# A gather of one activation is issued ahead of each added row, twelve rows ahead, in the v stage of a PEER layer

## The chip, the cores and the metric

The kernel runs on one core of a Trainium2 chip. The metric is the device time of one execution, in microseconds (us). TensorE is called PE here, its weight loads PEld, VectorE DVE, ScalarE ACT, GpSimd POOL and SyncE SP.

## The reference

A decoder trunk of two layers over 256 tokens of width 1024. Each layer is a mixer followed by a PEER feed-forward block, each behind a layer norm. Only the PEER block is touched. Per token it chooses 8 x 16 of 16384 experts; each expert has a row of `u` and a row of `v`, 1024 floats each:

```python
u_e = u[experts]
v_e = v[experts]
a = jax.nn.gelu(jnp.einsum("thkd,td->thk", u_e, xc), approximate=False)
return jnp.einsum("thk,thkd->td", (g * a).astype(v.dtype), v_e)
```

`experts` are the chosen indices, `g` their softmax weights.

## The kernel before

`peer(l)` runs once for each of the two layers. Its two long stages treat all experts densely, 128 of them a step:

- The **u stage** (128 steps) streams `p_u` and computes the activation of every expert for every token. For 192 of the 256 tokens these stay in the chip's memory and are multiplied there by the gates. For the last 64 tokens (`GT`) they go to a scratch table in device memory, `actD`, by a store of POOL every fourth step (line 735).
- The **v stage** (the loop over `j` at line 820, 128 steps) streams `p_v`, 512 KB a step, and multiplies it by the gated activations of those 192 tokens.

The 64 other tokens have 8 x 16 chosen experts each, 8192 (token, expert) pairs, laid out as 64 columns of 128 pairs. For each column c POOL issues two indirect DMAs: `g_act(c)` (line 456) gathers 128 single floats, the activations, from `actD` into one column of a small tile `gel`; `g_row(c)` (line 450) gathers 128 rows of `p_v`, 4 KB each, so 512 KB, into one of a ring of six tiles (`RING`). `g_mac(c)` (line 460) is DVE's: at every fourth column it multiplies four columns of `gel` by the gates into `gw` (line 462), then it adds row times weight to `gacc` (line 467), and then it has POOL issue `g_row(c + 6)` into the tile that it has just freed. The first six rows are gathered while the u stage runs.

In a v step, in program order: `nxt` prepares tiles two or three steps ahead (SP loads a `p_v` tile into one of eight buffers, `raw` or `spare`, line 92; ACT rounds it to `hi`, line 104; DVE subtracts for `lo`, line 115), `w_lo` and `w_hi` split the activations in the same way (lines 751 and 746), then the gathers and `g_mac` come, and last `v_mm`, ten matmuls of 128x512 (line 181; for the last eight steps four of the ten are put off to the end of the stage). A load into a buffer waits until DVE has finished with the tile that is in it, eight tiles back. Each engine works through its own list in program order.

Which step does what for the gathered columns: at step 0 `g_act(0)` to `g_act(3)` are issued, and at each step j from 1 to 60 `g_act(j + 3)`. The column gc is added at step 7 + int(113/64 x gc), so one column every 1.77 steps: column 0 at step 7, column 30 at step 59, column 51 at step 97, column 63 at step 118.

Of the kernel before, what the change touches and what calls it, by code (L numbers as in the profile page):

```python
# [35 lines left out]
GT = 64  # L36
ND = S - GT
RING, LEAD = 6, 7
GB = 0.8
GS = 2.0 ** 15  # L40


class Kern:
# [379 lines left out]
    def peer(self, l):  # L423
        tc, nc, I = self.tc, self.nc, self.I
        self.v0 = self.v0s.pop(0)
        with ExitStack() as es:
# [23 lines left out]
            def g_row(c):  # L450
                if c < P // 2:
                    t = grow[c] = gat.tile([P, D], F32, tag="row", name="row", bufs=RING)
                    nc.gpsimd.indirect_dma_start(out=t, out_offset=None, in_=gtable,  # L453
                                                 in_offset=bass.IndirectOffsetOnAxis(ap=gidx[:, 0, c:c + 1], axis=0))

            def g_act(c):
                nc.gpsimd.indirect_dma_start(out=gel[c // 4][:, c % 4:c % 4 + 1], out_offset=None, in_=gplaces,  # L457
                                             in_offset=bass.IndirectOffsetOnAxis(ap=gidx[:, 1, c:c + 1], axis=0))

            def g_mac(c):  # L460
                if c % 4 == 0:
                    nc.vector.tensor_tensor(gw[:, c:c + 4], gel[c // 4], ggate[:, c:c + 4], op=OP.mult)
                t = grow.pop(c)
                if c == 0:
                    nc.vector.tensor_scalar(gacc, t, gw[:, 0:1], None, op0=OP.mult)
                else:
                    nc.vector.scalar_tensor_tensor(gacc, t, gw[:, c:c + 1], gacc, op0=OP.mult, op1=OP.add)  # L467
                g_row(c + RING)
# [143 lines left out]
            def g_flush(n=1):  # L612
                if len(gq) < n:
                    return
                while gq:
                    t0, oi, gs = gq.popleft()
                    ps = self.acc(t0 // 4 % 2)
                    for q in range(4):
                        for w in range(2):
                            self.mm(ps[:, q * P:(q + 1) * P], oi[:, q // 2, :, q % 2], gs[w][:, q // 2, :, q % 2],  # L620
                                    w == 0, w == 1)
                    pv = ps.rearrange("p (t j) -> p j t", t=4)
                    k = done["a"]
                    for x, j0, n in A:
                        m = min(max(k, 0), n)
                        if m > 0:
                            y = x[:, 0:m, t0:t0 + 4]
                            nc.vector.scalar_tensor_tensor(y, pv[:, j0:j0 + m], 1.0 / GS, y, op0=OP.mult, op1=OP.mult)  # L628
                        if m < n:
                            nc.scalar.activation(x[:, m:n, t0:t0 + 4], pv[:, j0 + m:j0 + n], AF.Copy, scale=1.0 / GS)  # L630
                        k -= n
                    done["g"] = t0 + 4
# [3 lines left out]
            def run_side(budget):  # L636
                credit[0] = min(credit[0] + budget, 2 * budget)
                while credit[0] > 0 and side:
                    try:
                        cost = next(side[0])  # L640
                        if cost is None:
                            return
                        credit[0] -= cost
                    except StopIteration:
                        side.popleft()
# [67 lines left out]
            def u_fin(x):  # L713
                while due:
                    y, ps = due.popleft()
                    nc.vector.tensor_tensor(y, y, ps, op=OP.mult)
                if x is None:
                    return
                j, ps, wide = x
                jj = (P - FIRST + j) % P  # L720
                y, n = slot(jj), done["g"]
                if wide:
                    t = gat.tile([P, S], F32, tag="half", name="half", bufs=2)
                    nc.scalar.copy(t, ps[:, S:2 * S])  # L724
                    nc.vector.tensor_tensor(ps[:, 0:S], ps[:, 0:S], t, op=OP.add)  # L725
                if n:
                    nc.scalar.activation(ps[:, 0:n], ps[:, 0:n], AF.Gelu)  # L727
                    due.append((y[:, 0:n], ps[:, 0:n]))
                if n < ND:
                    nc.scalar.activation(y[:, n:ND], ps[:, n:ND], AF.Gelu)  # L730
                if j % 4 == 0:
                    gst.append(gat.tile([P, 4, GT], F32, tag="gst", name="gst", bufs=2))
                nc.scalar.activation(gst[-1][:, j % 4, :], ps[:, ND:S], AF.Gelu)  # L733
                if j % 4 == 3:
                    nc.gpsimd.dma_start(self.actD[:, jj - 3:jj + 1, :], gst.pop())  # L735
                done["a"] = j + 1
# [6 lines left out]
            def w_hi(j):  # L743
                if j < P:
                    WW[j] = late[0].tile([P, 3 * P], F32R, tag="w", name="W", bufs=10) if late else W[0][:, j % 5, :]
                    nc.scalar.copy(WW[j][:, 0:ND], slot(j))  # L746

            def w_lo(j):
                if j < P:
                    for o, c in ((2 * P, slice(0, P)), (ND, slice(P, ND))):  # L750
                        nc.vector.tensor_tensor(WW[j][:, o:o + c.stop - c.start], slot(j)[:, c],  # L751
                                                WW[j][:, c].bitcast(F32), op=OP.subtract)
# [8 lines left out]
            for j in range(P):  # L761
# [3 lines left out]
                g_flush(2)  # L765
                run_side(1.6 if len(A) == 1 else GB)
                if not side and len(A) == 1:
# [8 lines left out]
            while side or gq:  # L776
                g_flush()
                run_side(GB)
            u_fin(pu)
# [10 lines left out]
            def v_mm(j, tt, blocks, start=False, stop=False):  # L790
                hi, lo, w = kept[j]
                xh, xl, xm = w[:, 0:P], w[:, 2 * P:3 * P], w[:, P:2 * P]
                items = ((xm, hi), (xm, lo)) if tt else ((xh, hi), (xh, lo), (xl, hi))
                for a, (xx, ww) in enumerate(items):
                    go, end = start and a == 0, stop and a == len(items) - 1
                    for f in blocks:
                        self.mm(accs[tt][f], xx, ww[:, f * 512:(f + 1) * 512], go, end)

            rate, gc = (P - 8 - LEAD) / 64, 0
# [20 lines left out]
            for j in range(P):  # L820
                if j == P - FIRST:

                    es_1.close()
                    late.append(es.enter_context(tc.tile_pool(name="late", bufs=2 * NT - 6, reuse_waits="tile")))
                    for q in range(P - NT, P - 3):
                        self.alt[self.si + q - j] = lambda: [late[0].tile([P, D], F32R, tag="keep", name="keep") for _ in range(2)]
                hi, lo = self.nxt(j < P - 2)
                w_lo(j + 2)
                w_hi(j + 3)
                if j == NEXT + 1:  # L830
                    hN = self.reload_h()
                if j + 4 == P - 1:
                    gb = self.load_gb(2 * l + 1)
                kept[j] = (hi, lo, WW.pop(j))
                for c in range(4) if j == 0 else range(j + 3, min(j + 4, 64)):
                    g_act(c)
                if late_sums:
                    late_sums.popleft()()
                while gc < 64 and j >= LEAD + int(rate * gc):
                    g_mac(gc)  # L840
                    gc += 1
                    if gc in (60, 64):
                        late_sums.append((g_alpha, g_copy)[gc == 64])
                v_mm(j, 0, (0, 1), j == 0, j == P - 1)
                if j < P - NT:
                    v_mm(j, 1, (0, 1), j == 0)
                    kept.pop(j)
# [785 lines left out]
```

## Time and profile before

| | us |
|---|---|
| median of 3 runs (1788.25 to 1798.21) | 1792.02 |
| the profiled execution | 1791.22 |
| its span, first to last instruction | 1789.4 |
| v stage of layer 0, from | 557 |
| v stage of layer 1, from | 1468 |

The span is what the trace shows from the first to the last instruction. The two v stages are read by stretches of the trace: the stretches in which activations are gathered, and those after the last of these (710 us in layer 0, 1630 us in layer 1). Busy time of POOL holds its DMA issues as long as they take on the engine. "remote" as a releaser is an event from outside the engines; where the waiting instruction reads a loaded tile, it is the load.

### The profile page before, as it was taken

Reading aid. Unit: us, or ns where it says so; the run is one execution under the profiler, and the core shown is the slowest. Engines: PE = TensorE matmul, PEld = TensorE weight load, DVE = VectorE, ACT = ScalarE, POOL = GpSimd, SP = SyncE. Lnnn points to the kernel's source line nnn. Section 1 sums busy time; section 2 is a strip of 40 time slices with the busy share of each in tenths; the row PEclk is TensorE's granted clock in tenths of the full one; section 3 lists DMA queues with packets and bytes.
Section 4 is the critical chain, followed back from the end, with each engine's and each line's share of the span. In section 5 each row is a group of like instructions: output and inputs, shape, how many; then the busy total and the mean of one; then the engine's idle time right before and its main releaser. Section 6 shows DMA issues by size and latency. Waiting matters only on the chain. (4 is left out here: it accounts for less than half of the span.)

```text
span 1789.4 us, 30937 instructions
## 1 busy us (share of the span) xinstructions
PE 1730.8 (97%) x10610; PEld 1489.2 (83%) x10610; DVE 1554.7 (87%) x3675; ACT 1042.2 (58%) x2267; POOL 494.5 (28%) x441
## 2 busy tenths in 40 slices
PE   7999999999999999999897999999999999989997
PEld 6879999888888867888785789998888887768886
DVE  6778988989997989999768779988899987879998
ACT  6646455666666545556457755556666665445553
POOL 2110002000003777661431210020000007766630
PEclk9999999999999999999999999999999999999999
DMA  7445657555557999997671365666555558989992
GB/s 257 158 144 177 201 172 271 189 178 179 183 174 256 368 316 344 377 375 277 220 229 53 101 219 185 197 203 238 182 177 176 187 190 324 345 297 354 378 371 92
DMA packets 120654, 416.69 MB, mean 233 GB/s; under 512 B 18065, under 2 KB 20145, under 8 KB 119409
## 3 DMA queue, kind: packets, MB, share of 16 engines
q1 hardware_dynamic: 91008, 322.61, 53.6%
q0 software_dynamic: 29488, 92.10, 13.9%
q8 instruction: 84, 1.38, 0.3%
q14 instruction: 74, 0.60, 0.1%
HBM read 400.49 MB, written 13.63 MB: 231 GB/s over the span
## 5 line engine op out<-in xcount | busy, mean ns | idle before, releaser
L181 PE MATMUL mm<-hT,hi 128*128 128x256 f32 (+1 forms) x3360 | 838.6, 330 | 0.0
L181 PE MATMUL mm<-hT,lo 128*128 128x256 f32 x2376 | 638.2, 281 | 1.1 <-DVE lo L115 1.0
L104 ACT CAST hi<-raw 128x1024 fp32r<-128x1024 f32 (+1 forms) x463 | 484.2, 1048 | 255.2 <-PE acc L181 87.3
L115 DVE TENSOR_TENSOR lo<-raw,hi 128x1024 fp32r<-128x1024 f32 (+1 forms) x459 | 559.1, 1221 | 44.0 <-ACT hi L104 32.6
L181 PEld LDWEIGHTS mm<-hT,hi 128*128 128x128 f32 x3360 | 552.2, 188 | 49.3 <-issue 1.2
L181 PEld LDWEIGHTS mm<-hT,lo 128*128 128x128 f32 x2376 | 448.3, 189 | 15.5 <-DVE lo L115 1.9
L181 PE MATMUL acc<-hi,W 128*128 128x512 f32 x1476 | 419.6, 392 | 6.3 <-issue 4.7
L181 PEld LDWEIGHTS acc<-hi,W 128*128 128x128 f32 x1476 | 276.8, 188 | 71.5 <-issue 11.7
L181 PE MATMUL acc<-lo,W 128*128 128x512 f32 x984 | 307.3, 393 | 7.1 <-issue 4.7
L453 POOL DMA_INDIRECT row<-p_v,gidx x128 | 220.8, 1725 | 132.8 <-DVE gacc L467 90.7
L735 POOL DMA_DIRECT2D actD<-gst x64 | 34.9, 546 | 794.5 <-ACT gst L733 794.5
L181 PEld LDWEIGHTS acc<-lo,W 128*128 128x128 f32 x984 | 183.3, 188 | 54.8 <-issue 10.2
L104 ACT CAST hi<-spare 128x1024 fp32r<-128x1024 f32 x126 | 132.3, 1050 | 139.9 <-PE acc L181 101.7
L115 DVE TENSOR_TENSOR lo<-spare,hi 128x1024 fp32r<-128x1024 f32 x126 | 153.7, 1220 | 26.7 <-issue 16.9
L457 POOL DMA_INDIRECT gel<-actD,gidx x128 | 148.1, 1157 | 51.5 <-issue 37.8
L467 DVE SCALAR_TENSOR_TENSOR gacc<-row,gw,gacc 128x1024 f32<-128x1024 f32 x126 | 161.3, 1280 | 1.1
L727 ACT ACTIVATE mm<-mm 128x192 f32<-128x192 f32 (+23 forms) x170 | 40.9, 241 | 122.5 <-DVE mm L725 122.5
L751 DVE TENSOR_TENSOR W<-A,W 128x128 fp32r<-128x128 f32 (+1 forms) x512 | 107.5, 251 | 1.8 <-ACT W L746 1.8
L746 ACT CAST W<-A 128x192 fp32r<-128x192 f32 x256 | 88.3, 346 | 0.0
L725 DVE TENSOR_TENSOR mm<-mm,half 128x256 f32<-128x256 f32 x174 | 74.4, 428 | 15.1 <-ACT half L724 14.7
L628 DVE SCALAR_TENSOR_TENSOR A<-acc,A 128x176 f32<-128x176 f32 (+16 forms) x268 | 55.9, 274 | 34.7 <-PE acc L181 31.7
L730 ACT ACTIVATE A<-mm 128x192 f32<-128x192 f32 (+23 forms) x244 | 67.7, 277 | 7.1 <-DVE mm L725 2.0
(275 smaller groups left out, 1755.1 us busy)
## 6 DMA issues: line engine op xcount, KB each, us to landing
raw<-p_u SPq DMA_DIRECT2D x256, 512.0 KB
raw<-p_v SPq DMA_DIRECT2D x128, 512.0 KB
spare<-p_v SPq DMA_DIRECT2D x128, 512.0 KB
raw<-p_wq SPq DMA_DIRECT2D x32, 512.0 KB
actD<-gst POOLq DMA_DIRECT2D x64, 128.0 KB
raw<-b_wo SPq DMA_DIRECT2D x12, 512.0 KB
raw<-a_wo SPq DMA_DIRECT2D x8, 512.0 KB
raw<-s_wT SPq DMA_DIRECT2D x8, 512.0 KB
```

The costliest lines, as they stand in the source:

```text
L104: self.nc.scalar.copy(self.his[i], self.raws[i])
L115: e.tensor_tensor(self.los[i], raw, self.his[i].bitcast(F32), op=OP.subtract)
L181: self.nc.tensor.matmul(out, a, b, start=start, stop=stop)
L453: nc.gpsimd.indirect_dma_start(out=t, out_offset=None, in_=gtable, in_offset=bass.IndirectOffsetOnAxis(ap=gidx[:, 0, c:c + 1], axis=0))
L457: nc.gpsimd.indirect_dma_start(out=gel[c // 4][:, c % 4:c % 4 + 1], out_offset=None, in_=gplaces, in_offset=bass.IndirectOffsetOnAxis(ap=g ...
L467: nc.vector.scalar_tensor_tensor(gacc, t, gw[:, c:c + 1], gacc, op0=OP.mult, op1=OP.add)
L628: nc.vector.scalar_tensor_tensor(y, pv[:, j0:j0 + m], 1.0 / GS, y, op0=OP.mult, op1=OP.mult)
L725: nc.vector.tensor_tensor(ps[:, 0:S], ps[:, 0:S], t, op=OP.add)
L727: nc.scalar.activation(ps[:, 0:n], ps[:, 0:n], AF.Gelu)
L730: nc.scalar.activation(y[:, n:ND], ps[:, n:ND], AF.Gelu)
L746: nc.scalar.copy(WW[j][:, 0:ND], slot(j))
L751: nc.vector.tensor_tensor(WW[j][:, o:o + c.stop - c.start], slot(j)[:, c], WW[j][:, c].bitcast(F32), op=OP.subtract)
```

## The change

A constant `AHEAD = 12` is added, and the place of the activation gathers in the v loop is changed. The number of instructions and of DMAs stays, and so does the order of the rows.

```diff
-                for c in range(4) if j == 0 else range(j + 3, min(j + 4, 64)):
+                for c in range(2 * j, 2 * j + 2) if j < AHEAD // 2 else ():
                     g_act(c)
                 if late_sums:
                     late_sums.popleft()()
                 while gc < 64 and j >= LEAD + int(rate * gc):
+                    if gc + AHEAD < 64:
+                        g_act(gc + AHEAD)
                     g_mac(gc)
                     gc += 1
```

Steps 0 to 5 now issue two activation gathers each (columns 0 to 11), and from step 7 on one is issued ahead of each `g_mac`, for the column twelve further on; the last, column 63, at step 97.

## Rows read from the trace of the kernel before

**Rows 1.** Engines over the whole span: busy us (share) x instructions (page, part 1).
```profile
PE 1730.8 (97%) x10610; PEld 1489.2 (83%) x10610; DVE 1554.7 (87%) x3675; ACT 1042.2 (58%) x2267; POOL 494.5 (28%) x441
```

**Rows 2.** Matmul line 181, by stretch: length, PE, PEld busy (count), clock, DMA, GB/s.
```profile
557.00:640.00 83.00, 83.00 (x366) 68.29 (x365) 1.00 0.96 353
640.00:710.00 70.00, 65.55 (x269) 48.90 (x268) 1.00 0.92 322
710.00:840.00 130.00, 130.00 (x575) 107.62 (x575) 1.00 0.97 361
1490.00:1630.00 140.00, 131.00 (x535) 99.96 (x535) 0.98 0.90 317
1630.00:1760.00 130.00, 130.00 (x575) 107.65 (x574) 1.00 0.95 355
...
750.00:760.00 10.00, 10.00 (x46) 8.28 (x45) 1.00 1.01 406
...
1600.00:1610.00 10.00, 6.49 (x15) 3.69 (x16) 0.73 0.65 200
```

**Rows 3.** Timeline of PE, undisturbed stretch: start us, length us, instruction, count.
```profile
723.86 1.07 PE L181 MATMUL acc<-hi,W 128*128 128x512 f32 x4
...
726.13 1.07 PE L181 MATMUL acc<-hi,W 128*128 128x512 f32 x4
```

**Rows 4.** Waits, 640 to 710 us: total us, times, longest us.
```profile
ACT hi L104 <- remote: 8.9, 5, 3.1
```

**Rows 5.** Waits, 1490 to 1630 us.
```profile
ACT hi L104 <- remote: 22.8, 7, 6.6
```

**Rows 6.** Waits, 1630 to 1740 us: no activation gathers left.
```profile
ACT hi L104 <- PE acc L181: 47.3, 48, 2.0
POOL row L453 <- DVE gacc L467: 41.6, 26, 2.8
```

**Rows 7.** Timeline of layer 1, start of its v stage; idle before in brackets.
```profile
1489.41 0.16 DVE L462 TENSOR_TENSOR gw<-gel,ggate 128x4 f32<-128x4 f32 x1 [5.13 <-DMA gel<-actD,gidx]
...
1503.69 1.05 ACT L104 CAST hi<-spare 128x1024 fp32r<-128x1024 f32 x1 [6.60 <-remote]
```

**Rows 8.** Waits of SP's queue, 555 to 850 us.
```profile
SPq L92 <- DVE W L751: 205.4, 95, 4.5
```

**Rows 9.** Line 453 alone, 710 to 810 us: length, POOL busy (count), clock, DMA.
```profile
710.00:810.00 100.00, 67.70 (x26) 1.00 0.99 376
```

**Rows 10.** DMA of 640 to 710 us, then of 1490 to 1630 us.
```profile
DMA packets 7123, 22.55 MB, mean 322 GB/s; under 512 B 1632, under 2 KB 1632, under 8 KB 7117
...
gel<-actD,gidx POOLq DMA_INDIRECT x29
...
DMA packets 13780, 44.32 MB, mean 317 GB/s; under 512 B 3115, under 2 KB 3115, under 8 KB 13642
...
gel<-actD,gidx POOLq DMA_INDIRECT x56
```

**Rows 11.** Timeline of POOL: packed stretch, act-free stretch, the longest activation gather.
```profile
604.33 1.03 POOL L457 DMA_INDIRECT gel<-actD,gidx  x1 [0.30 <-DMA row<-p_v,gidx]
605.67 0.97 POOL L453 DMA_INDIRECT row<-p_v,gidx  x1 [0.30 <-issue]
...
741.04 3.51 POOL L453 DMA_INDIRECT row<-p_v,gidx  x1 [0.65 <-DVE gacc L467]
...
1574.88 3.85 POOL L457 DMA_INDIRECT gel<-actD,gidx  x1 [0.31 <-issue]
```

**Rows 12.** Busy us of all engines (instructions), clock, DMA share, GB/s: 580 to 600.
```profile
580.00:600.00 20.00, 20.00 (x90) 16.57 (x89) 19.96 (x34) 11.14 (x19) 15.92 (x15) 1.00 0.94 341
```

**Rows 13.** Groups of the page: count, busy us, mean ns, idle before and releaser.
```profile
L453 POOL DMA_INDIRECT row<-p_v,gidx x128 | 220.8, 1725 | 132.8 <-DVE gacc L467 90.7
...
L457 POOL DMA_INDIRECT gel<-actD,gidx x128 | 148.1, 1157 | 51.5 <-issue 37.8
```

More of the change, by code (lines that the diff above doesn't have):

```diff
@@ L38 @@
 RING, LEAD = 6, 7
+AHEAD = 12
 GB = 0.8
```

## The prediction

> **What bounds the kernel now.** I read the page's engine table first: PE is busy for 97% of the span, DVE for 87% [rows 1]. So time can only come from where PE stands still. The second view is the matmuls of line 181 by stretches of the two v stages [rows 2]. An undisturbed step takes PE 2.27 us, from the start of a group of four matmuls to that of the next step's [rows 3], so 0.227 us for each of its ten. At that pace 640 to 710 us would hold 308 matmuls and holds 269: 39 are missing, 8.9 us. 1490 to 1630 us would hold 617 and holds 535: 82 are missing, 18.6 us. The stretches after the last activation gather (710 to 840, 1630 to 1760) hold 575 in 130 us, which is the full pace, and so does 557 to 640. So PE loses 27.5 us in the two v stages, all of it while activations are being gathered. A part of the 18.6 us is the clock: from 1600 to 1610 the mean granted clock is 0.73, so some of it was spent at 1.2 instead of 2.4 GHz, right after PE had stood still.
>
> The third view is the waits of those stretches. ACT's rounding of a loaded `p_v` tile waits for the load: 8.9 us in layer 0 [rows 4], 22.8 us in layer 1 [rows 5]. After the last activation gather it waits only for PE to free `hi` tiles, at most 2.0 us at a time [rows 6]. So the late thing is the `p_v` load. Loads are late for two reasons that the trace can't wholly part. First, the DMA engines have more to do than a step has time for. Second, when DVE stands still, loads are issued late: at step 7 of layer 1 it waits 5.13 us for the first four activations, and 14 us later ACT waits 6.60 us for a load [rows 7]; SP's queue waits nearly always for DVE to free a buffer [rows 8].
>
> **The DMA's price list.** A step loads 0.524 MB of `p_v` and on average 64/113 = 0.566 of a row gather of the same size: 0.821 MB, 362 GB/s at 2.27 us. The best ten undisturbed microseconds moved 406 GB/s [rows 2], a whole stretch without activation gathers, where nothing waited for a load, 376 [rows 9]. So the capacity lies between 376 and 406; I take 390, the middle, since the first is a demand that was met, not a limit, and the second a short peak. While loads are late the DMA is the limit, and what the bytes don't explain is the price of the activation gathers: 22.55 MB and 29 gathers in 70 us, 44.32 MB and 56 gathers in 140 us [rows 10]. At 390 GB/s that is (70 - 57.8)/29 = 0.42 and (140 - 113.6)/56 = 0.47 us a gather, say 0.45. At 376 GB/s it is 0.35 and 0.40, at 406 GB/s 0.50 and 0.55.
>
> **The change part by part.** No DMA, instruction or byte is added or taken away. What moves is when the 64 activation gathers of a layer are issued. Before, some 57 steps (4 to 60) carry one each. After, steps 0 to 5 carry twelve, and 52 follow at 0.566 a step, to step 97. By step 60 the old order has issued 64, the new one 12 + 31 = 43; 21 gathers a layer move into steps 61 to 97, where PE now loses nothing.
>
> Demand on the DMA in a step, at 390 GB/s: bytes 2.105 us; before + 0.45 = 2.555, so 0.285 over PE's 2.27, and 16.2 us over 57 steps. After: 2.105 + 0.566 x 0.45 = 2.36, so 0.09 over, and 8.3 us over the 92 steps from 6 to 97. In layer 0 PE lost 8.9 of the 16.2 us; the other 7.3 were swallowed by the tiles loaded ahead. So layer 0 should lose 8.3 - 7.3 = 1.0, a gain of 7.9 us. Layer 1 lost 18.6, 2.4 more than the 16.2; with the same 2.4 on top it should lose 10.7, a gain of 7.9 again. Together 15.8, say 16 us.
>
> Bounds, by the same sum: at 376 GB/s (0.375 a gather; 2.184 us of bytes) before is 0.289 over and after 0.126, 16.5 against 11.6 us: 4.9 a layer, so 10. At 406 GB/s (0.525; 2.022) 15.8 against 4.5: 11.3 a layer, but no more than the 8.9 there are in layer 0: 20. Of the clock I count nothing apart; it is in the 18.6.
>
> The Trainium skill (HBM Reference, Specifications and the lines below its table) puts a core that streams alone at about 425 GB/s, and its share when the neighbour streams too at about 358. The second would say that no step of this stage fits, and the 376 GB/s above speak against that; by the first an activation gather would cost 0.61 us and the same sum would give a gain of 24 us.
>
> POOL's queue: in the packed stretch it issues one gather after the other with 0.30 us between (the activation gather at 604.33, the row at 605.67) [rows 11], and is busy for 15.92 of 20 us with 15 of them [rows 12]; with 15 gaps of 0.30 that is all it has. The change takes this load off: two gathers per column, each column 4.01 us (1.77 steps). The new activation gather stands ahead of `g_row(c + 6)`; it waits for nothing itself (indices and table are ready), so it delays the row by its own length at most, and it runs in the time in which POOL waited for `gacc` (41.6 us in rows 6). At the start thirteen activation gathers instead of eleven stand ahead of the first row: 2 x 1.36 = 2.7 us later. That row is read ten steps, 23 us, after its tile is freed; these cover it, and without them the cost is the 2.7 us. The first four activations can't land earlier than now, since the table's last store decides when POOL starts; so I leave the 5.13 us of rows 7 in. Later ones are issued at least nine columns, 36 us, ahead of their use in `gw`; an empty cover would cost DVE such a wait again. SP's queue is not passed by anything.
>
> The profiled execution took 1791.2 us; 1791.2 - 15.8 = 1775.4, and the median stands 0.8 above it: 1776.
>
> **The rivals.**
> *All of it goes.* If the tiles loaded ahead swallow the 8.3 us in both layers, and the 2.4 us and the slow clock of layer 1 are only followers of its first stall, the full 27.5 us come back: 1764. For it: layer 0 ran 83 us at full pace with a gather in every step. Against it: the 5.13 us wait at step 7 is left where it is, and late loads follow it.
>
> *The stall only moves, or was not the gathers'.* Steps 61 to 97 may have no room: there the DMA's share reads 0.99 [rows 9]. Then 21 x 0.45 = 9.5 us a layer are taken from the first half and given back in the second. Or the late loads come mainly from the loop of DVE, SP and load once DVE has been held up. Either way the gain is 0 to 8 us: 1784 to 1792. For it: that 0.99. Against it: DVE, held up before, is catching up in that stretch and so asks for more than PE's pace; and no stall of either layer lies behind the last activation gather.
>
> *POOL becomes the bound, and it gets slower.* In the stretch without activation gathers a row takes POOL 67.7/26 = 2.60 us, up to 3.51, while DVE is busy without a gap; the longest activation gather took 3.85 [rows 11]. If the activation gathers cost 2.60 there too, a column needs 2 x 2.60 + 0.60 = 5.80 us against 4.01. Over the 21 columns from step 61 to 97 POOL falls 37.6 us behind; the ring covers five columns, 20 us, and DVE waits for rows for the other 17.6 in each layer, PE behind it: 1792 + 35 = 1827. It decides from (4.01 + 20/21) = 4.96 us a column. Against it: the means over all, 1.73 for a row and 1.16 for an activation [rows 13], and the row at its 2.60 give 4.36, which the ring covers; and POOL gets through 15 gathers in 20 us at 1.06 each while DVE is busy for 19.96 of them [rows 12]. The Trainium skill (SBUF — State Buffer, Who interferes with whom) says that a DVE instruction with two SBUF inputs holds up a GpSimd instruction that reads SBUF, until it ends. DVE's work here is of that kind, so the page speaks for this rival; rows 11 agree with it in the longer gathers, and rows 12 show that it doesn't set the pace.
>
> **How the numbers follow.** Chances: the forecast with its bounds (10 to 20 us, 1772 to 1782) 0.47; all of it goes 0.15; the stall moves or stays 0.30; POOL 0.08. Half a per cent, about what a measurement of this kernel can tell from no change, is 9 us: faster means under 1783, slower over 1801. The first two cases are faster, 0.62; the third is the same, 0.30; POOL is slower, 0.08. The range takes in the first three cases but for the ends of two of them: 1763 to 1796; what is left out is POOL's and the tails.
>
> **What would show it.** Right: the matmuls of layer 0's stage run near full pace throughout; layer 1 keeps a stall near step 15, behind DVE's wait for the first activations; ACT's waits for loads shrink to less than half; POOL waits for `gacc` from the first columns on instead of issuing without pause; stretches behind step 61 keep their ten matmuls per 2.27 us. Wrong: PE stalls between steps 61 and 97, with loads late there (it moved); stalls of the old size in the first half with fewer gathers in them (they were not the cause); DVE waiting for `row` and POOL's gathers at over 2.5 us each (POOL).

## The result and the profile after

| | before | after |
|---|---|---|
| median, us | 1792.08 | 1771.2 |
| lowest to highest | 1788.25 to 1798.21 | 1761.58 to 1772.26 |
| the profiled execution | 1791.22 | 1771.35 |
| its span | 1789.4 | 1769.5 |
| v stage of layer 0, of layer 1, from | 557, 1468 | 557, 1460 |

The ratio after to before is 0.987, with an interval of 0.982 to 0.991: 21 us less, where 16 were forecast, and inside the range. One of the four executions after took 1761.58 us, the other three 1771 to 1772. Every ratio in this document is against the kernel before in the same session on the same chip. In three sessions of experiments that kernel had a median of 1790 to 1792; in the last one it took 1757 to 1762, and the changed kernel was not run there (see the last experiment). In the second of these sessions one of its 25 executions took 4015 us and is left out. So the 1.3% holds where the kernel before has the stalls that [rows 2] show.

Line numbers are one higher after: 182 for the matmul, 105 and 116 for `hi` and `lo`, 454 for the row, 458 for the activation, 463 for `gw`, 468 for the sum.

The engine table of after, against [rows 1]: PE has the same work and ten microseconds less busy time, POOL is busy 12 us longer.

```profile
PE 1720.8 (97%) x10610; PEld 1491.2 (84%) x10610; DVE 1552.9 (88%) x3675; ACT 1042.6 (59%) x2267; POOL 506.9 (29%) x441
```

The matmuls of line 182 by stretches, as in [rows 2]: length, PE, PEld (count), clock, DMA share, GB/s.

```profile
557.27:640.00 82.73, 82.73 (x366) 68.53 (x365) 1.00 0.96 364
640.00:710.00 70.00, 70.00 (x310) 57.98 (x309) 1.00 0.96 355
710.00:840.00 130.00, 130.00 (x576) 107.66 (x575) 1.00 0.93 347
1460.24:1480.00 19.76, 19.76 (x89) 16.34 (x88) 1.00 0.94 360
1480.00:1510.00 30.00, 27.56 (x109) 19.55 (x108) 1.00 0.81 287
1510.00:1630.00 120.00, 120.00 (x531) 99.36 (x530) 1.00 0.98 369
```

The second line had 269 matmuls before and has 310, the full pace. In layer 1 only the 30 us from 1480 are short of matmuls: 109, where 133 would be the full pace, 5.4 us. The other lines of both stages run at 2.27 us a step.

The waits of 640 to 710 us, then of 1450 to 1630 us (total, times, longest), against [rows 4, 5]:

```profile
ACT hi L105 <- PE acc L182: 23.3, 22, 3.7
POOL row L454 <- DVE gacc L468: 4.1, 2, 3.1
...
DVE gw L463 <- DMA gel<-actD,gidx: 5.0, 1, 5.0
ACT hi L105 <- remote: 2.3, 1, 2.3
ACT hi L105 <- DMA spare<-p_v: 2.2, 3, 1.0
```

ACT waited 8.9 us for loads in the first stretch; now no such line is left, it waits for PE. In layer 1 the 22.8 us have become 2.3 and 2.2. DVE's wait for the first four activations is there as it was. What it leads to stands in the timeline of after (start, length, instruction; idle before in brackets), against [rows 7]:

```profile
1481.23 0.16 DVE L463 TENSOR_TENSOR gw<-gel,ggate 128x4 f32<-128x4 f32 x1 [4.98 <-DMA gel<-actD,gidx]
...
1489.02 1.05 ACT L105 CAST hi<-spare 128x1024 fp32r<-128x1024 f32 x1 [5.05 <-PE acc L182]
1495.45 1.05 ACT L105 CAST hi<-spare 128x1024 fp32r<-128x1024 f32 x1 [5.13 <-PE acc L182]
1499.04 1.05 ACT L105 CAST hi<-raw 128x1024 fp32r<-128x1024 f32 x1 [2.30 <-remote]
```

POOL's groups of the page (count, busy us, mean ns, idle before and releaser), against [rows 13]:

```profile
L454 POOL DMA_INDIRECT row<-p_v,gidx x128 | 209.8, 1639 | 101.3 <-DVE gacc L468 40.0
L458 POOL DMA_INDIRECT gel<-actD,gidx x128 | 172.3, 1346 | 50.9 <-issue 37.8
```

Four of its gathers from the timeline, against [rows 11]:

```profile
662.67 3.84 POOL L458 DMA_INDIRECT gel<-actD,gidx  x1 [0.30 <-issue]
666.82 3.84 POOL L454 DMA_INDIRECT row<-p_v,gidx  x1 [0.30 <-issue]
670.97 1.09 POOL L458 DMA_INDIRECT gel<-actD,gidx  x1 [0.30 <-issue]
672.36 1.02 POOL L454 DMA_INDIRECT row<-p_v,gidx  x1 [0.30 <-DVE lo L116]
```

### The profile page after: what moved, and what is told of

It reads as the page before. It is cut to its first block, busy times and chain, and to the rows that moved or that the text cites. A ratio compares the mean times of both kernels' runs of the same rounds, so it can differ in the third digit from the quotient of the medians.

```text
span 1769.5 us, 30968 instructions
## 1 busy us (share of the span) xinstructions
PE 1720.8 (97%) x10610; PEld 1491.2 (84%) x10610; DVE 1552.9 (88%) x3675; ACT 1042.6 (59%) x2267; POOL 506.9 (29%) x441
## 4 chain that ended last, share of the span: by engine, by line
PE 71%; issue 13%; DVE 8%; DMA 3%; ACT 2%; POOL 2%; POOLq 0%; ACTq 0%; DVEq 0%; SPq 0%
PE mm L182 35%; PE acc L182 34%; DVE lo L116 1%; PE mm L211 1%; DMA actD<-gst 1%; POOL gel L458 1%; DMA raw<-p_wq 1%; DMA raw<-s_wT 1%; POOL row L454 1%; ACT hi L105 1%; DVE bnst L257 1%; POOL actD L736 1%; DVE hN L279 0%; DVE hN L261 0%; DVE hN L254 0%
## 5 line engine op out<-in xcount | busy, mean ns | idle before, releaser
L182 PE MATMUL acc<-hi,W 128*128 128x512 f32 x1476 | 415.1, 389 | 0.8 <-issue 0.6
L454 POOL DMA_INDIRECT row<-p_v,gidx x128 | 209.8, 1639 | 101.3 <-DVE gacc L468 40.0
L458 POOL DMA_INDIRECT gel<-actD,gidx x128 | 172.3, 1346 | 50.9 <-issue 37.8
L629 DVE SCALAR_TENSOR_TENSOR A<-acc,A 128x176 f32<-128x176 f32 (+16 forms) x268 | 56.0, 274 | 34.5 <-PE acc L182 31.5
```

What stands on the lines that cost most here:

```text
L182: self.nc.tensor.matmul(out, a, b, start=start, stop=stop)
```

## The experiments

Four accounts of the late loads were set against each other. *Load*, the prediction's: the bytes and small packets of the gathers are more than the DMA can move in a step. *Hold-up*: DVE, once late, frees buffers late, SP loads late, ACT waits. *POOL*: its queue is overfull and rows come late. *Indirect gathers*: too many of them per step make the loads land late, though the transfers leave the DMA engines time (perhaps because some of the 16 fall behind; that is a guess, as no trace here tells the 16 apart). The table counts what PE lost, in us: for each stretch of 45.4 us (20 steps) from the start of the stage, the matmuls missing from the 201 or 202 that an undisturbed one holds, times 0.227. These counts come from the one profiled execution of each kernel, which can lie off the median (e4's took 1782.57 us). e2, e3 and f2 ran twice each, the others four times or more.

| kernel | median, us | ratio [95%] | layer 0, steps 0-20-40-60-80-100 | layer 1 |
|---|---|---|---|---|
| before | 1792 | | 0, 1.9, 6.7, 1.2, 0 | 5.3, 2.6, 6.7, 4.2, 0 |
| after | 1771 | 0.987 [0.982, 0.991] | 0, 0, 0, 0, 0 | 5.1, 0.3, 0, 0, 0 |
| e1 no activation gathers | 1761 | 0.984 [0.979, 0.989] | 0, 0, 0, 0, 0 | 0, 0, 0, 0, 0 |
| e2 small loads by SP | 1768 | 0.989 [0.982, 0.995] | 3.5, 0, 0, 0, 0 | 6.2, 0.6, 0, 0, 0 |
| e4 before, half rows | 1792 | 1.001 [0.998, 1.004] | 0, 5.6, 1.9, 3.1, 0 | 6.2, 3.7, 1.9, 4.2, 0 |
| f1 one POOL add a step | 1780 | 0.993 [0.991, 0.996] | 0, 0, 1.7, 2.8, 4.2 | 0.8, 0.1, 0, 2.8, 4.9 |
| f2 before, plain activations | 1764 | 0.985 [0.981, 0.988] | 0, 0, 0, 0, 0 | 0, 0, 0, 0, 0 |
| f3 extra gathers late | 1790 | 1.000 [0.997, 1.002] | 0.8, 0.6, 0, 2.2, 3.3 | 6.5, 1.0, 0, 1.7, 7.2 |
| e6 before, first row at step 10 | 1786 | 0.997 [0.995, 0.999] | 0, 9.6, 2.6, 0.6, 0 | 0, 0.3, 11.5, 0, 0 |
| g1 before, adjacent floats | 1815 | 1.013 [1.009, 1.017] | 2.8, 8.1, 1.2, 12.1, 0 | 5.1, 1.7, 10.8, 11.9, 0 |
| g2 before, plain rows | 1770 | 0.988 [0.985, 0.992] | 0.6, 0, 1.9, 0.6, 0 | 0, 0.6, 2.6, 1.2, 0 |
| e5 after, first row at step 10 | 1763 | 0.984 [0.981, 0.986] | 0, 0, 0, 0, 0 | 0, 0, 0, 0, 0 |

**How much is there: e1.** The changed kernel without any activation gather.

```diff
-                for c in range(2 * j, 2 * j + 2) if j < AHEAD // 2 else ():
-                    g_act(c)
+                if j == 0:
+                    for x in gel:
+                        nc.gpsimd.memset(x, 0.5)
...
-                    if gc + AHEAD < 64:
-                        g_act(gc + AHEAD)
```

> The changed kernel with all 128 activation gathers left out; the small tiles that they fill get one constant instead, so the 64 last tokens' sums are not the reference's. Theory of load (an activation gather costs the DMA engines some 0.45 us, and one a step is more than a step has room for): what the gathers cost in all is what is left to gain, and the changed kernel still lost some 5 us near step 15 of layer 1, behind DVE's wait for the first four activations; that wait is gone too, so both v stages run at full pace, 0.227 us a matmul, and the time is 1764 to 1768 us. Theory of the queue (rows late behind POOL's activation gathers): the same. Theory of the hold-up (the stalls come from DVE standing still once, not from the gathers' load): the same in time, but then the capacity that remains should show no better GB/s than before. If stalls are left with no gather at all, all three are wrong, and rows and loads alone are too much.

1760.73 us, and no loss in either stage. So with the gathers at their new places some 10 us are left of what they cost, the wait for the first of them included, and about 30 us was all there was.

**Load: e2 and e4.** One adds small packets where the stall was, the other takes bytes away from there. e2 has SP load 128 single floats in each of the steps 4 to 60 of the changed kernel:

```diff
+                if 4 <= j <= 60:
+                    t = gat.tile([P, 1], F32, tag="small4", name="small4", bufs=8)
+                    nc.sync.dma_start(t, self.actD[:, j, 0:1])
```

> The changed kernel, and SP loads 128 single floats from the same table into a small tile at each of the steps 4 to 60 that nobody reads (57 small loads a layer, on SP's queue, none on POOL's). Theory of load: with 1.57 small transfers a step the stalls of the first half come back, at 0.45 us each 2.105 + 0.705 = 2.81 us a step, 0.54 over for 57 steps, 31 us a layer less the 7 swallowed: some 45 us in all, over 1800 us; at a third of that price still 10 us. Theory of the queue: POOL's work is as in the changed kernel, so the stalls stay away, 1770 us. Theory of the hold-up: no stall but the one near step 15 of layer 1, 1770 us.

1768.1 us, less than the changed kernel's own median. What is lost (3.5 and 6.8 us) is lost in the first steps, at the wait for the first activations; the old stalls of steps 20 to 80 didn't come back. The matmuls of 640 to 710 us, then the DMAs issued there:

```profile
640.00:710.00 70.00, 70.00 (x310) 57.98 (x309) 1.00 1.02 370
```

```profile
small<-actD SPq DMA_DIRECT2D x27, 0.5 KB
gel<-actD,gidx POOLq DMA_INDIRECT x19
row<-p_v,gidx POOLq DMA_INDIRECT x18
```

Here are 46 transfers of 128 floats in 70 us, where the kernel before had 29 [rows 10], at full pace and with the DMA's share at 1.02. e4 halves the rows of the kernel before (2 KB each, used twice; the sums of the last 64 tokens change):

```diff
-  indirect_dma_start(out=t, out_offset=None, in_=gtable, ...
+  indirect_dma_start(out=t[:, 0:512], out_offset=None, in_=ghalf, ...
```

> The kernel before, but each row gather fetches half a row (128 x 2 KB), and DVE reads that half twice, so its work is as long; the sums of the 64 last tokens are not the reference's. POOL issues exactly as many gathers in the same order as before. Theory of load: the bytes of a step fall to 0.673 MB, 1.73 us at 390 GB/s, and with one activation gather 2.18 us, under PE's 2.27: no stall in the first half but what DVE's wait for the first activations leaves in layer 1, so 1765 to 1772 us. Theory of the queue: POOL is as packed as before and rows as late in being issued, so 1785 us or more. Theory of the hold-up: the loop starts as before, some 5 us less at most, 1785 us.

The time stayed, 1792.22, and so did stalls of 10.6 and 16.0 us, with the DMA well under what it can do (matmuls by stretch, as above):

```profile
640.00:710.00 70.00, 67.86 (x287) 52.72 (x286) 1.00 0.82 274
1490.00:1630.00 140.00, 131.03 (x549) 100.97 (x548) 1.00 0.82 274
```

So the load account fell: neither bytes nor small packets make these loads late. The trace of before could have told it. Its queue table for 600 to 690 us (packets, MB, share of the 16 engines) has the software queue, with 39 activation gathers and 22 rows in it, at 34.5 / 11.59 = 2.98% a MB, and the loads' queue at 60.7 / 19.37 = 3.13%:

```profile
q1 hardware_dynamic: 5326, 19.37, 60.7%
q0 software_dynamic: 4431, 11.59, 34.5%
```

At 0.45 us of all engines the 39 gathers would have held 19.5% by themselves. So their packets take next to no engine time. What an engine may lose between two packets stands in no share.

**POOL: e3 and f1.** Work for POOL is added to each of the steps 4 to 60 of the changed kernel, four small adds or one:

```diff
+                if 4 <= j <= 60:
+                    for _ in range(4):
+                        nc.gpsimd.tensor_tensor(busy, busy, busy, op=OP.add)
```

> The changed kernel, and POOL does four small additions on a tile of its own at each of the steps 4 to 60, some 1 to 1.5 us of its time a step and no transfer, so that its queue is as full as in the kernel before. Theory of load: nothing comes back, 1768 to 1773 us. Theory of the queue: rows are issued late again, the stalls of the first half come back, 1785 to 1795 us. Theory of the hold-up: 1770 us.

> The changed kernel, and POOL does one small addition on a tile of its own (128x64, some 0.5 us with its gap) at each of the steps 4 to 60: POOL is about as full as in the kernel before (1.13 gathers of 1.36 us and this addition, 2.1 us of a step of 2.27), with no more transfers than in the changed kernel. Theory of POOL's fullness: the old stalls come back, PE loses 15 us or more in the first halves, 1785 us or more. Theory of stragglers (an indirect gather that POOL issues holds up some of the 16 DMA engines, whatever its bytes; at 1.57 of them a step the slowest engine falls behind, at 1.13 not): nothing comes back, 1766 to 1773 us. Theory of load by bytes or small packets: fallen by the half rows and the small loads on SP; it would say 1770.

e3 took 1956.31 us (ratio 1.094 [1.086, 1.102]), far above what any account had forecast: the four adds took 2.1 us a step (0.52 each), not 1 to 1.5. It is the prediction's third rival in the flesh, POOL as the bound: DVE waits for rows, with the longest sum of all its waits (waits over the whole span):

```profile
DVE gacc L471 <- DMA row<-p_v,gidx: 170.6, 42, 7.3
```

f1, at 1780.04, lies between the two forecasts. POOL issues without a pause from 590 to 718, with 61 gathers in 128 us, and nothing is lost up to step 40, 1.3 us in the whole stretch. POOL manages 30 columns there, 4.27 us each where 4.01 are wanted, and falls behind, until at 718 DVE waits 2.1 us for a row. Then POOL catches up: 19 gathers in the next 24 us, one in 1.26 us. PE loses 4.0 us there and 1.9 more up to 750 (all engines by stretch: PE, PEld, DVE, ACT, POOL, then clock, DMA share, GB/s; last, from the waits of 690 to 760 us, DVE's for rows):

```profile
590.00:718.00 128.00, 126.51 (x558) 104.10 (x557) 124.70 (x204) 72.22 (x111) 111.74 (x114) 1.00 0.96 353
718.00:742.00 24.00, 20.88 (x88) 15.90 (x87) 18.15 (x31) 7.27 (x12) 18.52 (x19) 1.00 1.00 378
...
DVE gacc L471 <- DMA row<-p_v,gidx: 2.1, 1, 2.1
```

So a packed POOL by itself costs little as long as its gathers come at 1.08 a step. Whether the larger stall is the late row's or that of the gathers in close order, f1 can't part.

**Indirect gathers: f2 and f3.** f2 fetches the activations of the kernel before by plain DMAs of POOL, at the old places, with the same 128 floats of four bytes (other ones, so that the last 64 tokens' sums change):

```diff
-  indirect_dma_start(out=gel[c // 4][:, c % 4:c % 4 + 1], out_offset=None, in_=gplaces, ...
+  dma_start(gel[c // 4][:, c % 4:c % 4 + 1], self.actD[:, c, 0:1])
```

> The kernel before, but each activation gather is a plain DMA of the same shape on POOL's queue (128 single floats, one from each row of the table; not the chosen ones, so the 64 last tokens' sums are not the reference's). POOL has as many DMAs in the same order, 0.55 us instead of 1.16 for these. Theory of stragglers, if it is POOL's descriptors of whatever kind: stalls as before, 1785 us or more. Theory of stragglers, if it is the indirect ones alone: only 0.57 indirect gathers a step are left, no stall but layer 1's near step 15, 1765 to 1772 us. Theory of POOL's fullness: 0.57 x 1.36 + 0.85 = 1.6 us of a step, not full, 1765 to 1772 us.

1763.83, and nothing is lost. POOL's queue holds as many DMAs as before, but two more things differ: the addresses are evenly spaced, and POOL is busy 0.57 us with a plain activation DMA, 1.16 with a gather. Matmuls of 600 to 690 us, then the DMAs issued there (count, KB each):

```profile
600.00:690.00 90.00, 90.00 (x399) 74.53 (x398) 1.00 1.00 369
```

```profile
gel<-actD POOLq DMA_DIRECT2D x41, 0.5 KB
row<-p_v,gidx POOLq DMA_INDIRECT x23
```

f3 puts more indirect gathers, one every second step, into steps 61 to 97 of the changed kernel:

```diff
+                if 61 <= j <= 97 and j % 2 == 0:
+                    t = gat.tile([P, 1], F32, tag="extra", name="extra", bufs=8)
+                    c = j - 40
+                    nc.gpsimd.indirect_dma_start(out=t, ..., in_offset=...(ap=gidx[:, 1, c:c + 1], axis=0))
```

> The changed kernel, and one more activation gather into a tile that nobody reads at every second step from 61 to 97 (18 a layer), so that these steps carry 1.63 indirect gathers each, as many as the first half did before. If the rate of gathers decides and not the place: PE stalls in steps 61 to 97, some 0.29 us a step over 37 steps, 10 us a layer less the 7 that the loads ahead swallow, so 3 to 10 us a layer, 1777 to 1790 us. If the first half is special (DVE has just been held up there, rows and loads begin together): no stall there, 1768 to 1773 us.

1790.16: the whole gain is gone. PE loses 5.5 us in layer 0 and 8.9 in layer 1 in steps 60 to 100, where the changed kernel lost nothing. DVE waits for no row in either stage, so it isn't POOL's lateness. The stall goes where the gathers go: at 39 indirect ones from 700 to 760 us, 1.48 a step (before: 61 from 600 to 690, 1.54 a step), it comes; at 49 from 600 to 690 (after, 1.24 a step) it doesn't. Matmuls of f3's 700 to 760 us, where 264 would be the full pace, then the gathers issued there:

```profile
700.00:760.00 60.00, 59.06 (x257) 47.59 (x256) 1.00 0.95 341
...
row<-p_v,gidx POOLq DMA_INDIRECT x14
gel<-actD,gidx POOLq DMA_INDIRECT x13
extra<-actD,gidx POOLq DMA_INDIRECT x12
```

**Which of it: g1, g2.** Both are the kernel before. g1's gathers read 64 adjacent floats:

```diff
-  tensor_scalar(t2[u, 1, :], t2[u, 1, :], float(GT), self.tokg[u], op0=OP.mult, op1=OP.add)
+  tensor_scalar(t2[u, 1, :], t2[u, 1, :], 0.0, self.tokg[u], op0=OP.mult, op1=OP.add)
```

> The kernel before, in which the 128 indices of each activation gather all point to 64 adjacent floats of the table (the token's own place in its first 64 entries) instead of being spread over 4 MB. So many gathers of the same kind, at the same places in the order; the sums of the last 64 tokens are not the reference's. If the spread of the addresses over device memory makes the gathers dear, the stalls go and the time falls to that of plain DMAs, 1764 (1758 to 1772). If it is the number of indirect gathers per step, nothing changes: 1785 to 1796, and layer 0 loses about 9 us between 600 and 700 as before. I take the second.

Neither: it got slower, 1815.25, with 24 and 29 us lost, at the same number of gathers; the DMA's share fell to 0.73 in 640 to 710 us, where it was 0.92 (matmuls of that stretch):

```profile
640.00:710.00 70.00, 64.67 (x259) 47.94 (x257) 0.98 0.73 281
```

So where a gather reads matters, and its price isn't time that the DMA engines are busy. g2 loads the rows plainly and leaves the activations indirect, one a step:

```diff
-  indirect_dma_start(out=t, out_offset=None, in_=gtable, ...
+  dma_start(t, I["p_v"][l, 2 * c])
```

> The kernel before, with the rows of p_v loaded by plain DMAs of POOL (one whole expert tile of 128 rows of 4 KB) in place of indirect gathers; the bytes, the packet size and the queue stay, the sums of the last 64 tokens are not the reference's. Activation gathers stay indirect, one a step from step 4 to 60, so 1.0 indirect gather a step in place of 1.57. If the rate of indirect gathers decides, whatever they fetch, this is below the 1.13 a step at which the changed kernel lost nothing: no loss in steps 20 to 60, 1762 to 1772. If it is the activation gathers at one a step as such (their 128 four-byte packets), the stalls stay: 1782 to 1794. I take the first.

1770.29: of the 28.6 us 7.5 are left. That is the direction of the expectation, but not nothing; and a part is of another kind, as DVE now waits for rows (560 to 720 us):

```profile
DVE gacc L466 <- DMA row<-p_v: 7.7, 5, 2.8
```

**Hold-up: e6 and e5.** The first row is added at step 10 in place of 7, in the kernel before and in the changed one, so that DVE asks for the first activations 6.8 us later:

```diff
-RING, LEAD = 6, 7
+RING, LEAD = 6, 10
```

> The kernel before with LEAD 10 instead of 7: the first row is added three steps later, so that DVE finds the first four activations there; the rows are added at one in 1.72 steps instead of 1.77. Theory of the hold-up (DVE stands still once, loads are issued late, and a loop of DVE, SP and load keeps it going): without the 3.2 and 5.1 us waits the stalls of both layers shrink by more than half, 1770 to 1778 us. Theory of stragglers: only what follows the wait directly goes, some 5 us in layer 1, and at most that in layer 0; 1783 to 1792 us.

> The changed kernel with the first added row at step 10 in place of 7 (and the rate of columns adapted by the same formula), so that DVE asks for the first four activations three steps, 6.8 us, later. Nothing is left out. In the changed kernel DVE waits 5.0 us for them in layer 1 and PE loses 5 us behind that. If that wait is the cause, it goes and so do the 5 us: 1764 to 1768 against the changed kernel's 1771. If PE's loss is an effect of the twelve gathers issued at once at the start of the stage, it stays: 1769 to 1773. The steeper rate of columns (64 in 110 steps in place of 113) raises the indirect gathers from 1.13 to 1.16 a step, which should cost nothing. I take the first, 1766.

In e6 the wait is gone and layer 1's first stretch with it (5.3 to 0), but the other stalls move about and stay the same in sum (23.3 before, 24.6): 1785.59. Hold-up is worth some 5 us and isn't the cause of the rest. The traces say so too. In the kernel before SP issues a load 0.03 us (median) after DVE has freed its buffer, and the loads that ACT waits for in layer 0 had been issued 14 to 24 us ahead, so they were late to land. One of them, its issue, its use by ACT, and all engines in the time between:

```profile
639.67 0.33 SPq L92 DMA_DIRECT2D spare<-p_v  x1
663.67 1.05 ACT L104 CAST hi<-spare 128x1024 fp32r<-128x1024 f32 x1 [1.58 <-remote]
...
639.67:663.67 24.00, 20.95 (x80) 13.79 (x79) 15.78 (x28) 9.11 (x15) 18.21 (x16) 1.00 0.92 321
```

The packets of some eight loads went through in these 24 us, so this one stood in the DMA's queue for most of them, and still the engines' share was 0.92, at 321 GB/s.

In e5 the 5 us are all that was left: no loss anywhere, 1762.90 (1758.81 to 1765.40), ratio 0.984 [0.981, 0.986], the best of the versions that leave nothing out. The interval overlaps that of the changed kernel (0.982 to 0.991), so it is the trace that shows the 5 us gone. Its timeline has no idle time ahead of the first `gw`, and its matmuls keep their pace behind it:

```profile
1479.47 0.16 DVE L463 TENSOR_TENSOR gw<-gel,ggate 128x4 f32<-128x4 f32 x1
```

```profile
1480.00:1510.00 30.00, 30.00 (x134) 24.85 (x133) 1.00 0.90 324
```

**Indirect or uneven: g4.** The plain DMAs of f2 read evenly spaced floats. g4 reads the same floats by indirect gathers, in the kernel before:

```diff
-  tensor_scalar(t2[u, 1, :], t2[u, 1, :], float(GT), self.tokg[u], ...)
+  tensor_scalar(t2[u, 1, :], self.iota4[u, 0, :, 0], 1.0 / P, self.tokg[u], ...)
+  for hh in range(2):
+      o = slice(hh * 64, hh * 64 + 64)
+      tensor_scalar(t2[u, 1, o], t2[u, 1, o], float(P * GT), hh * 64.0 * (P * GT - GT), ...)
```

> The kernel before, in which column c's activation gather reads the same 128 floats as the plain DMA did (entry 8192 p + 64 c for partition p, evenly spread over the 4 MB), but by an indirect DMA, its indices prepared beforehand. The sums of the last 64 tokens are not the reference's. The kernel with 64 adjacent floats showed that the place of the addresses has a price (1815), so two theories are left for why the plain DMAs lost nothing: that they were not indirect, or that their addresses lay evenly. If indirect gathers as such are dear at 1.57 a step, this stays at 1785 to 1796 with 9 us lost in layer 0 and 18 in layer 1. If the chosen experts' uneven addresses make the gathers dear, the losses go and it falls to 1760 to 1772. I take the second, at three in five.

1759.46 against 1759.61, ratio 1.000 [0.999, 1.001]. The kernel before, which the theories had at 1790, took 1757 to 1762 in all the 13 runs made beside g4. The question is not answered, since there was nothing to lose. But the trace of g4 says something else: 600 to 690 us hold 40 and 23 indirect gathers, as many as stall the kernel before, and the matmuls are at full pace. Half of the loads land within 6.6 us of their issue (DMAs with their median us from issue to landing).

```profile
600.00:690.00 90.00, 90.00 (x399) 74.53 (x398) 1.00 1.01 380
```

```profile
spare<-p_v SPq DMA_DIRECT2D x21, 512.0 KB, 6.6
gel<-actD,gidx POOLq DMA_INDIRECT x40, 6.2
row<-p_v,gidx POOLq DMA_INDIRECT x23, 7.3
```

If even places were what helped, the kernel before, with its uneven ones, would have stalled beside it; it didn't. So the number of gathers a step is not enough by itself for a stall: something outside the kernel, that differed between sessions, has to come with it. What that is, no trace here shows; other work on the chip, or the place of the tensors in device memory, are two candidates that no run tests. This chip is the one on which e1 to e4 ran, with the kernel before at 1790 then, so it isn't the chip alone.

## Why the prediction was right, and where not

**The bound and the prize: right.** 27.5 us were read off as lost, all while activations are gathered. e1, f2 and e5, which lose nothing, stand 27 to 30 us below the kernel before of their sessions.

**The mechanism: half right.** That the gathers are too many in steps 4 to 60 and that steps 61 to 97 have room for 21 more was the argument, and after shows it: nothing lost in either half of layer 0. f3 finds the end of that room, at half a gather a step more. What failed is the step "what the bytes don't explain is the price of the activation gathers", 0.45 us of the DMA's capacity. Loads did stand in the DMA's queue, landing up to 24 us after their issue, so the DMA was what they waited for. But the time that the bytes leave over is not the gathers' own: in 640 to 710 us the share was 0.92 [rows 2], and e4, with half the bytes of the rows, stalls as much at 0.82, where the same division (19.20 MB and 28 gathers in 640 to 710 us) gives 0.74 us a gather. I took idle time of engines with loads queued for a price of each gather. e2 shows that small packets issued by SP cost nothing after the first steps, and the queue table of before has the time of POOL's. What leaves the engines idle stays open.

**The size: term by term.** A linear price left 0.09 us a step over and so 1.0 us lost in layer 0 and 10.7 in layer 1. Measured were 0 and 5.4: at 1.24 indirect gathers a step the loss is not smaller but absent, as for a threshold. The stages gained 9.8 and 13.4 us where 7.9 each were forecast; the spans differ by 19.9, so some 3 us are lost again outside these counts. That the forecast came within 5 us is in part luck: it started from the losses in [rows 2], which were read rightly, but the price that divided them was wrong. By the Trainium skill's 425 GB/s (HBM Reference, Specifications and the lines below its table) the same sum gave 24 us, nearer to the 21; that is no support for it, as the sum's form is what fell, and the 406 GB/s of [rows 2] lie below it.

**What was left alone: right.** The 5.13 us wait for the first activations was to stay, with late loads behind it: it is 4.98, and the only loss of the changed kernel follows it, within 30 us. e5 shows that this wait is the cause.

**POOL: right, by less than it looked.** The two gathers a column got through: 1.64 + 1.35 + 0.60 = 3.59 us against 4.01, and DVE waits for no row. Single gathers of 3.84 us come up in a row (662.67, 666.82), and POOL makes up for them at 1.0 to 1.1 each. The forecast that POOL would wait for `gacc` from the first columns on held poorly: 4.1 us in 640 to 710. The rule that a DVE instruction with two SBUF inputs holds up such instructions of POOL (the Trainium skill, SBUF — State Buffer, Who interferes with whom), which spoke for the rival, set no pace here: 3.59 us a column against 4.01. The rival's threshold of 4.96 us a column holds for the 21 columns it was worked out for; f1, at 4.27 over 30 columns, paid 9 us. By the rival's own sum POOL was then 7.8 us behind, within the 20 that the ring was to cover, and yet DVE waited for rows, 4.8 us in layer 0. So the cover was less than the 20 us.

**The rivals.** "All of it goes" (1764) came true one edit later, in e5 (1762.9). "The stall only moves" fell: no stall in steps 61 to 97. Its second form, the loop of DVE, SP and load, is worth the 5 us of layer 1's start; elsewhere the loads were late to land.

**Open.** Why the gathers delay loads that stand in the queue while the DMA engines are partly idle; whether uneven addresses are needed for it; and what outside the kernel switched the stalls off in the last session. What the change does in such a session was not measured: the kernel before is then as fast as e5 in the others.

## What to carry to other kernels

Before a stall beside a busy DMA is priced in bytes or packets, read the queue table of the same stretch: time per MB of each queue tells whether the suspected transfers hold the engines at all. Then take a late load's issue and its use: they tell whether it was issued late or landed late. Here, in every session but the last, indirect gathers at some 1.5 a step went with loads that landed late, and at 1.24 they didn't, though their own packets took next to no time. So it is worth trying to spread such gathers to the pace of their use, and to let the first use come some steps after the first gather. Run the kernel before again in another session before a gain that rests on late loads is booked as fixed.

## What was not expected of the hardware

- A gather of 128 floats by an indirect DMA cost PE time where a plain one of the same size, in the same queue at the same places, cost none: 1791 against 1764 us (two executions; the plain one's addresses were evenly spaced).
- A load of 512 KB landed 24 us after its issue while the DMA engines' share was 0.92; in the session without stalls the median was 6.6 us.
- Gathers whose 128 addresses lie in 256 bytes were worse than scattered ones: 1815 against 1791 us, with the DMA's share down from 0.92 to 0.73.
- The same program took 1790 us in one session and 1760 in another on the same chip, steady within each (1781 to 1796, 1757 to 1762).
